# The query projection of a cross-attention as one Strassen step with streamed operands, in a fused decoder block on one Trainium2 core

## The chip, the cores and the metric

The program runs on one core of a Trainium2 chip. The metric is device time in microseconds of one execution, the median of the runs; the profile is one further execution with the hardware profiler on. The engines are TensorE (PE in the profile, its weight loads as PEld), VectorE (DVE), ScalarE (ACT), GpSimd (POOL) and SyncE (SP), whose queue issues nearly all DMAs.

## What is computed

A decoder block over 1024 tokens of width 1024 in float32: a mixer of a state-space branch and a gated linear attention branch, then cross-attention to 256 memory tokens, then a SwiGLU feed-forward layer, each behind an RMSNorm and with a residual sum. The part that matters here:

```python
merged = sigmoid(g_ssd) * (y_ssd @ w_up_ssd) + sigmoid(g_gla) * (y_gla @ w_up_gla)
h = h + merged @ w_o                       # 1024 x 1024
n = rmsnorm(h, norm_xattn)
q = (n @ w_xq).reshape(S, 4, 256)          # the query projection, 1024 x 1024
k, v = split(rmsnorm(mem, norm_mem) @ w_xkv, 2)
p = softmax(q @ k * 256 ** -0.5)
h = h + (p @ v) @ w_xo
```

## The kernel before

Activations lie transposed: 128 channels on the partitions, tokens along the free dimension, in two halves of 512 tokens (j = 0, 1). All matmuls of the projections are float32r with split operands: an operand x is kept as a rounded high part (a copy by ACT) and a low part (x minus the high part, by DVE), and a product is three matmuls, high x high, high x low and low x high. `split` makes such a pair, `into` makes one from a PSUM bank into an input slot.

Four dense 1024 x 1024 products of this part run one after another through `dense`: w_up_ssd, w_up_gla, w_o and w_xq, then, after the attention, w_xo. `dense(no, ins, post, pre)` runs over 8 blocks of 128 output channels and both token halves. Each of the 16 outputs is one PSUM bank ("acc", four of them) that takes 8 input blocks x 3 matmuls of 512 columns. The weights come from `Left` (lines 1190 to 1219): units of 256 output channels are loaded whole into "aux" buffers (1 MB each), and split, 128 channels at a time, into a ring of two buffers "wd" of the pool "m", two outputs ahead of use.

The output of w_o becomes the residual stream: `residual` adds the old one, stores it (h1_d), gives it to `put_xq` (lines 1365 to 1369) and squares it for the norm's statistics (`Stats.take`: the square on ACT into one buffer "sq", the running sum "ssum" on POOL or DVE, whichever of the two a meter kept at build time has free first). `put_xq` scales by the norm's gain and makes the high and the low part, the input i_xq of the query projection. The query projection writes its 8 output blocks, again split, into i_q, from which the attention takes scores. The factor of the norm itself, one number per token, is applied later, to the scores.

Beside the main work run side jobs, written as generators that `run` advances a step at a time. `presum` (lines 1297 to 1318) is the one that matters: it prepares sums of quadrants of w_ffn_out for the Strassen step of the last layer. Each of its 11 passes loads 1 MB into one buffer "pre" of the pool "m", makes four sums of 128 x 512 on POOL and stores each to down_d. It starts in the product of w_up_ssd and has steps until the query projection; down_d is read only by the down projection at the end.

Buffers of 8 KB per partition come from three pools by name: "op" (14), "aux" (4) and "m" (4). An input of a dense product takes 8 of them (`EVEN`: all "op"; `ODD`: six "op" and two "aux"). "ga" (6 of 2 KB) holds the residual's blocks and the raw keys and values. PSUM has 8 banks, four "acc" and four "bank".

The order on each queue is set at build time by a scheduler that follows the program's order as a priority and simulates the engines; work of a later step is drawn forward where its inputs and buffers are there. `ahead()` raises the priority of the instructions in it by 200 places. A queue then waits in order: an instruction that waits holds all that stand behind it on its engine.

The down projection of the feed-forward layer (lines 1568 to 1714) is already a Strassen step of the form that the change uses: seven products, in each of which both operands are streamed, and four banks filled side by side.

Of the kernel before, what the change touches and what calls it, by code (L numbers as in the profile page):

```python
# [10 lines left out]
F32R = mybir.dt.float32r  # L11
# [5 lines left out]
P = 128  # L17
# [61 lines left out]
def block_kernel(ctx: ExitStack, tc: tile.TileContext, t: dict, out: bass.AP):  # L79
# [19 lines left out]
    def dram(name, *shape):  # L99
        return dr.tile(list(shape), F32, name=name, tag=name)  # L100
# [14 lines left out]
    yg_d = dram("yg_d", D, TOK)  # L115
    act_d = dram("act_d", 7 * D_FF // 2, HALF)
    down_d = dram("down_d", 4 * D_FF // 2, HALF)
    kT_d = dram("kT_d", D, MEM)
    vm_d = dram("vm_d", MEM, D)
    cs_d = dram("cs_d", P, P)  # L120
# [1069 lines left out]
    class Left:  # L1190
# [2 lines left out]

        def __init__(s, mats):
            s.seq, s.raw, s.w, s.ring = [(W, u) for W in mats for u in range(4)], [], [], []

        def load(s, n):
            while len(s.raw) < min(n, len(s.seq)):
                W, u = s.seq[len(s.raw)]
                r = slot("aux", (P, NB, 256), name="raw")  # L1200
                SP.dma_start(r, W[:, 256 * u:256 * u + 256].rearrange("(k p) c -> p k c", p=P))
                s.raw.append(r)

        def upto(s, n):
            while len(s.w) < min(n, 2 * len(s.seq)):
# [12 lines left out]
            s.upto(n + 2)  # L1218
            return s.w[n]

    left = Left((t["w_up_ssd"], t["w_up_gla"], t["w_o"], t["w_xq"], t["w_xo"]))

    def paired(keys):

        return [(lambda k=k: slot(k, (P, 2, TOK), F32R, name="hl")) for k in keys]

    def hl(slots_, k):
        if callable(slots_[k]):
            slots_[k] = slots_[k]()
        return slots_[k]  # L1230

    def into(slots_, k, j, src, e=None):
        x = hl(slots_, k)
        split(src, x[:, 0, half(j)], x[:, 1, half(j)], e)
# [18 lines left out]
            yield  # L1253

    EVEN, ODD = ("op",) * 8, ("op",) * 6 + ("aux",) * 2
    i_ys, i_yg, i_wo, i_xq, i_q, i_xo = (paired(x) for x in (EVEN, ODD, EVEN, ODD, EVEN, EVEN))

    def fetch(src, dst, gain=None):

# [37 lines left out]
    def presum():  # L1297


        r = slot("m", (P, 2, D), name="pre")  # L1300
        for k in range(KP):
            SP.dma_start(r, t["w_ffn_out"][256 * k:256 * k + 256, :].rearrange("(j p) c -> p j c", p=P))
            yield
            a = lambda i, j: r[:, j, half(i)]
            s1_ = sums["m"].tile([P, HALF], F32, name="sa", tag="sa", bufs=2)
            put = lambda n, ap: SP.dma_start(down_d[(n * KP + k) * P:(n * KP + k + 1) * P, :], ap)
# [12 lines left out]

    def quad_of(src):  # L1320
        return lambda o, j: quad(src, o * P, 0, j)
# [35 lines left out]
    def residual(store, stats, gain, put, scale=1.0):  # L1357
# [4 lines left out]
            stats.take(j, q)  # L1362
        return post

    def put_xq(o, j, q, g):
        x = hl(i_xq, o)
        h, l = x[:, 0, half(j)], x[:, 1, half(j)]
        ACT.activation(h, q, AF.Copy, scale=g)
        DVE.scalar_tensor_tensor(l, q, g, h, ALU.mult, ALU.subtract)

    def waiting(g, n):
        for _ in range(n):
# [35 lines left out]
    drain(early)  # L1408
    load_kv(0)
    u_xo_stats = Stats(rp)  # L1410
# [126 lines left out]
    for n, _ in enumerate(dense(4, i_xo, residual(h2_d, u_xo_stats, "norm_ffn", put_xo), quad_of(h1_d), js=(1, 0))):  # L1537
# [213 lines left out]
```

## Time and profile before

| | |
|---|---|
| median of 3 runs | 1946.77 us (1946.58 to 1947.56) |
| span of the profiled execution | 1949.0 us |
| TensorE busy | 1916.2 us, 98% |
| DVE, ACT, POOL busy | 1298.5, 845.8, 557.8 us |
| moved by DMA | 317.98 MB, mean 163 GB/s |

The profile's page has the span and busy times, then groups of instructions by line, engine and operation (count, busy us, mean ns, and the idle time of the engine ahead of them with what ended it). L73 is the line of a helper through which all DVE and POOL instructions go, L51 the helper of all matmuls and L227 the one that makes high parts, so groups are told apart by their tiles: "hl" are split inputs, "wd" split weights of the dense products, "fs" split operands of the down projection, "pre" and "sa" the pre-sums. In a row of the order of time stand the start, the length, the engine, line and tiles, and in brackets how long the engine had idled and what ended that. All times in the trace are from the span's start. The query projection's matmuls lie between about 1075 and 1157 us.

### The profile page before, as it was taken

To read this page: it belongs to the slowest core of one execution; us is meant where nothing else is said; L and a number is where in the kernel's file an instruction comes from. 1 tells how busy PE (TensorE), PEld (TensorE's weight loads), DVE (VectorE), ACT (ScalarE), POOL (GpSimd) and SP (SyncE) were. 2 spreads that over 40 slices of the span, in tenths; PEclk is the share of its full clock that TensorE was granted. 3 is DMA by queue.
4 is the path that set the end of the run, shared out by engine and by line. 5 is a ranking of instruction groups with operands and counts; after the bars stand their busy time and mean duration, and the time that the engine had idled before them with its cause. 6 is when DMAs were issued, how large, how long until landed. Compare 5 with 4: busy or idle time off the path is not lost.

```text
span 1949.0 us, 26264 instructions
## 1 busy us (share of the span) xinstructions
PE 1916.2 (98%) x9776; PEld 1615.6 (83%) x9776; DVE 1298.5 (67%) x1873; ACT 845.8 (43%) x1485; POOL 557.8 (29%) x428
## 2 busy tenths in 40 slices
PE   7999999999999999999999999999999999999998
PEld 7998787888878888788887888888888888888888
DVE  7766879877776764655534237677777777766566
ACT  7534564655553444643223235444333333345243
POOL 0012334345543231022433000006445544320002
PEclk9999999999999999999999999999999999999999
DMA  9423383446553653997675201442233224177463
GB/s 341 144 93 101 130 307 107 152 161 186 174 173 123 198 167 124 348 346 270 226 269 164 82 22 44 140 141 82 90 126 110 82 100 144 42 271 239 157 224 126
DMA packets 237875, 317.98 MB, mean 163 GB/s; under 512 B 16538, under 2 KB 156036, under 8 KB 237748
## 3 DMA queue, kind: packets, MB, share of 16 engines
q1 hardware_dynamic: 236020, 310.01, 47.4%
q10 hardware_dynamic: 1728, 6.29, 0.8%
q8 instruction: 77, 1.26, 0.3%
q14 instruction: 50, 0.41, 0.1%
HBM read 215.27 MB, written 100.99 MB: 162 GB/s over the span
## 4 chain that ended last, share of the span: by engine, by line
PE 43%; DMA 3%; POOL 2%; DVE 1%; issue 1%; ACT 1%; POOLq 0%; SPq 0%; DVEq 0%; ACTq 0%
PE acc L51 38%; PE bank L51 4%; DMA pre<-in_w_ffn_out_dram 1%; POOL pre L73 1%; DMA down_d<-pre 1%; PE bank L55 1%; POOL ssum L73 0%; DVE hl L73 0%; POOL sa L73 0%; DMA h_d<-ga 0%; DMA ga<-vm_d 0%; DVE wd L73 0%; ACT wd L227 0%; ACT sq L493 0%; DVE phl L73 0%
## 5 line engine op out<-in xcount | busy, mean ns | idle before, releaser
L51 PE MATMUL acc<-hl,wd 128*128 128x512 f32 x1920 | 440.4, 390 | 3.6 <-DVE wd L73 2.0
L51 PEld LDWEIGHTS acc<-hl,wd 128*128 128x128 f32 x1920 | 359.6, 188 | 80.7 <-DVE wd L73 3.3
L73 DVE TENSOR_TENSOR wlo<-raw,whi 128x512 fp32r<-128x512 f32 x272 | 236.4, 875 | 103.6 <-ACT whi L227 103.5
L227 ACT ACTIVATE whi<-raw 128x512 fp32r<-128x512 f32 x272 | 169.5, 629 | 247.6 <-PE acc L51 201.0
L73 DVE TENSOR_TENSOR o<-acc,o 128x512 f32<-128x512 f32 (+1 forms) x256 | 172.6, 676 | 108.8 <-PE acc L51 95.4
L51 PE MATMUL acc<-fs 128*128 128x512 f32 (+1 forms) x792 | 155.7, 356 | 0.1
L51 PEld LDWEIGHTS acc<-fs 128*128 128x128 f32 x792 | 130.7, 189 | 20.8 <-issue 0.5
L73 DVE TENSOR_TENSOR fs<-fr,fs 128x1024 fp32r<-128x1024 f32 (+1 forms) x84 | 98.9, 1217 | 36.5 <-ACT fs L227 36.4
L227 ACT ACTIVATE fs<-fr 128x1024 fp32r<-128x1024 f32 (+1 forms) x84 | 79.2, 982 | 95.9 <-PE acc L51 31.2
L73 POOL TENSOR_TENSOR raw<-raw,sa 128x512 f32<-128x512 f32 x44 | 57.1, 1297 | 207.8 <-DVE wlo L73 207.8
L73 POOL TENSOR_TENSOR sa<-raw 128x512 f32<-128x512 f32 x43 | 69.6, 1619 | 107.0 <-DMA raw<-in_w_in_dram 78.9
L227 ACT ACTIVATE whi<-sa 128x512 fp32r<-128x512 f32 x96 | 59.6, 626 | 93.7 <-PE acc L51 92.3
L73 DVE TENSOR_TENSOR wlo<-sa,whi 128x512 fp32r<-128x512 f32 x96 | 80.9, 843 | 13.7 <-ACT whi L227 12.7
L73 DVE TENSOR_TENSOR wd<-raw,wd 128x1024 fp32r<-128x1024 f32 x40 | 52.8, 1323 | 47.6 <-ACT wd L227 47.2
L73 POOL TENSOR_TENSOR rstd<-rstd,mhalf 128x4 f32<-128x4 f32 (+1 forms) x7 | 8.7, 1246 | 257.0 <-DVE rstd L73 257.0
L227 ACT ACTIVATE wd<-raw 128x1024 fp32r<-128x1024 f32 x40 | 42.2, 1057 | 90.4 <-PE acc L51 89.8
L51 PE MATMUL acc<-T4h,whi 128*128 128x512 f32 x192 | 76.3, 397 | 2.4 <-DVE o L73 2.4
L51 PE MATMUL acc<-B22h,wlo 128*128 128x512 f32 x192 | 75.7, 394 | 1.5 <-DVE wlo L73 1.5
L51 PE MATMUL acc<-T1h,whi 128*128 128x512 f32 x192 | 76.3, 397 | 0.0
L51 PE MATMUL acc<-T2h,whi 128*128 128x512 f32 x192 | 75.9, 395 | 0.0
L51 PE MATMUL acc<-T3h,whi 128*128 128x512 f32 x192 | 75.9, 395 | 0.0
L51 PE MATMUL acc<-B22h,whi 128*128 128x512 f32 x192 | 75.7, 394 | 0.0
(399 smaller groups left out, 4698.6 us busy)
## 6 DMA issues: line engine op xcount, KB each, us to landing
raw<-in_w_in_dram SPq DMA_DIRECT2D x26, 1024.0 KB, 5.9
raw<-in_w_ffn_in_dram SPq DMA_DIRECT2D x22, 1024.0 KB, 6.5
act_d<-o SPq DMA_DIRECT2D x77, 256.0 KB, 2.1
fr<-act_d SPq DMA_DIRECT2D x35, 512.0 KB, 7.9
pre<-in_w_ffn_out_dram SPq DMA_DIRECT2D x11, 1024.0 KB, 10.0
fr<-down_d SPq DMA_DIRECT2D x20, 512.0 KB, 3.9
down_d<-pre SPq DMA_DIRECT2D x33, 256.0 KB, 3.1
h_d<-ga SPq DMA_DIRECT2D x32, 256.0 KB, 3.1
```

The lines of the kernel that those rows point to most:

```text
L51: return s.e.matmul(o, x, y, **kw)
L55: return s.e.transpose(o, x, i)
L73: return f(*a, **kw)
L227: ACT.activation(hi, src, AF.Copy)
```

## The change

The query projection is computed as one Strassen step (in Winograd's form) over quadrants of 512 x 512: seven products in place of eight, each with all 512 output channels of its half in four banks. w_xq is no longer one of `Left`'s matrices. The left operands are quadrants of w_xq or sums of them; the sums are made by `presum`, in four passes ahead of those over w_ffn_out, and stored in a new DRAM tensor xqs_d. The right operands are four quadrants of the input, which `put_xq` now stores unsplit in float32 (one scaled copy on ACT); DVE combines them in place, and both operands of every half product (two blocks of 128 channels) are split as they are needed, up to two half products ahead. Products that share terms add up in the same banks: B11, T2, T3 and T4 in four "acc" banks, T1 and B22 in four "bank" banks, B21 in four more. Three intermediate results are kept in "aux" buffers, and the four quadrants of the result go into i_q as before. `presum` is advanced two steps per half product in place of one per output. `Left` is held back at w_o's last unit until the twelfth step, when w_xo's units are freed.

```diff
+    xqs_d = dram("xqs_d", 2 * D, HALF)
...
+            s.limit = 12
...
-    left = Left((t["w_up_ssd"], t["w_up_gla"], t["w_o"], t["w_xq"], t["w_xo"]))
+    left = Left((t["w_up_ssd"], t["w_up_gla"], t["w_o"], t["w_xo"]))
...
-    i_ys, i_yg, i_wo, i_xq, i_q, i_xo = (paired(x) for x in (EVEN, ODD, EVEN, ODD, EVEN, EVEN))
+    i_ys, i_yg, i_wo, i_q, i_xo = (paired(x) for x in (EVEN, ODD, EVEN, EVEN, EVEN))
...
-        for k in range(KP):
-            SP.dma_start(r, t["w_ffn_out"][256 * k:256 * k + 256, :].rearrange("(j p) c -> p j c", p=P))
+        todo = [(t["w_xq"].rearrange("(j k p) c -> k p j c", j=2, p=P)[k], xqs_d, 4, k) for k in range(4)]
+        todo += [(t["w_ffn_out"][256 * k:256 * k + 256, :].rearrange("(j p) c -> p j c", p=P), down_d, KP, k)
+                 for k in range(KP)]
+        for src, dst, kn, k in todo:
+            SP.dma_start(r, src)
...
+    class Wide:
+        SEQ = ("B11", "T1", "B22", "T2", "B21", "T3", "T4")
+        LEFT = {"B11": (0, 0), "B21": (0, 1), "T1": 0, "B22": 3, "T2": 1, "T3": 2, "T4": (1, 1)}
+        COMB = {"T1": ((0, 0), (0, 1), (0, 0)), "T2": ((0, 0), (1, 1), (0, 0)), "T3": ((0, 1), (1, 1), (0, 1)),
+                "T4": ((1, 0), (1, 0), (0, 0))}
+        RIGHT = {"B11": (0, 0), "B22": (1, 1), "B21": (1, 0), "T1": (0, 0), "T2": (0, 0), "T3": (0, 1), "T4": (1, 0)}
...
+        def quad(s, i, j):
+            if (i, j) not in s.q:
+                s.q[i, j] = slot("op", (P, 4, HALF), name="rq")
+            return s.q[i, j]
...
+                r = slot(s.keys[len(s.raw)], (P, 4, HALF), name="wr")
+                SP.dma_start(r, w.rearrange("(k p) c -> p k c", p=P))
...
+        def prep(s, n):
+            while len(s.ops) < min(n, 14):
+                m, kp = divmod(len(s.ops), 2)
+                s.load(m + 1)
+                name, c = s.SEQ[m], slice(2 * kp, 2 * kp + 2)
+                x = [slot("op", (P, 2, 2, HALF), F32R, name="ws") for _ in range(2)]
+                with ahead():
+                    if name in s.COMB:
+                        o, a, b = (s.quad(*ij)[:, c] for ij in s.COMB[name])
+                        sub(DVE, o, a, b)
+                    split(s.raw[m][:, c], x[0][:, 0], x[0][:, 1])
+                    split(s.quad(*s.RIGHT[name])[:, c], x[1][:, 0], x[1][:, 1])
+                s.ops.append(x)
+        def evac(s, name, u, p):
+            with ahead():
+                if name in ("B11", "T1", "B22"):
+                    if name not in s.keep:
+                        s.keep[name] = slot(s.side, (P, 4, HALF), name="wk")
+                    ACT.activation(s.keep[name][:, u], p, AF.Copy)
+                elif name == "T4":
+                    s.post(1, 0, u, p)
+                else:
+                    k, i, j = {"T2": ("B22", 0, 1), "B21": ("B11", 0, 0), "T3": ("T1", 1, 1)}[name]
+                    o = s.keep[k][:, u]
+                    add(DVE, o, p, o)
+                    s.post(i, j, u, o)
+        def steps(s):
+            x = 0
+            for m, name in enumerate(s.SEQ):
+                if name in ("B11", "T1", "B21"):
+                    banks = [(acc if name == "B11" else bank)() for _ in range(4)]
+                    if name == "B11":
+                        s.chain = banks
+                elif name in ("T2", "T3", "T4"):
+                    banks = s.chain
+                fresh = name in ("B11", "T1", "B21")
+                for kp in range(2):
+                    s.load(m + 3)
+                    s.prep(x + 3)
+                    w, b = s.ops[x]
+                    for u in range(4):
+                        for k in range(2):
+                            for n, (a, c) in enumerate(((0, 0), (0, 1), (1, 0))):
+                                PE.matmul(banks[u], w[:, a, k, u * P:(u + 1) * P], b[:, c, k],
+                                          start=fresh and kp + k + n == 0, stop=kp + k == 2 and n == 2,
+                                          skip_group_check=True)
+                    x += 1
+                    if kp:
+                        for u in range(4):
+                            s.evac(name, u, banks[u])
+                    yield
+    xq = Wide(t["w_xq"], xqs_d, lambda i, j, u, p: into(i_q, 4 * i + u, j, p), ("aux", "op", "aux") * 3, "aux")
...
     def put_xq(o, j, q, g):
-        x = hl(i_xq, o)
-        h, l = x[:, 0, half(j)], x[:, 1, half(j)]
-        ACT.activation(h, q, AF.Copy, scale=g)
-        DVE.scalar_tensor_tensor(l, q, g, h, ALU.mult, ALU.subtract)
+        ACT.activation(xq.quad(o // 4, j)[:, o % 4], q, AF.Copy, scale=g)
...
-    run(dense(3, i_xq, lambda o, j, p, g: into(i_q, o, j, p)), (xq_side(), 1.0), (early, 1.0))
+    def next_left():
+        left.limit = len(left.seq)
+        left.upto(26)
+        yield
+    run(xq.steps(), (xq_side(), 1.0), (early, 2.0), (waiting(next_left(), 12), 1.0))
```

More of the change, by code (lines that the diff above doesn't have):

```diff
@@ L1195, in __init__ @@
             s.seq, s.raw, s.w, s.ring = [(W, u) for W in mats for u in range(4)], [], [], []
+            s.limit = 12
         def load(s, n):
-            while len(s.raw) < min(n, len(s.seq)):
+            while len(s.raw) < min(n, s.limit):
                 W, u = s.seq[len(s.raw)]
@@ L1204, in upto @@
         def upto(s, n):
-            while len(s.w) < min(n, 2 * len(s.seq)):
+            while len(s.w) < min(n, 2 * s.limit):
                 u, i = divmod(len(s.w), 2)
@@ L1305, in presum @@
             s1_ = sums["m"].tile([P, HALF], F32, name="sa", tag="sa", bufs=2)
-            put = lambda n, ap: SP.dma_start(down_d[(n * KP + k) * P:(n * KP + k + 1) * P, :], ap)
+            put = lambda n, ap: SP.dma_start(dst[(n * kn + k) * P:(n * kn + k + 1) * P, :], ap)
             add(POOL, s1_, a(1, 0), a(1, 1))
@@ L1363, in residual, with __init__, load @@
         return post
+    class Wide:
[4 more added lines that the diff above has]
+        RIGHT = {"B11": (0, 0), "B22": (1, 1), "B21": (1, 0), "T1": (0, 0), "T2": (0, 0), "T3": (0, 1), "T4": (1, 0)}
+        def __init__(s, W, sums_d, post, keys, side):
+            s.W, s.sums_d, s.post, s.keys, s.side = W, sums_d, post, keys, side
+            s.q, s.raw, s.ops, s.keep, s.chain = {}, [], [], {}, None
+        def quad(s, i, j):
+            if (i, j) not in s.q:
+                s.q[i, j] = slot("op", (P, 4, HALF), name="rq")
+            return s.q[i, j]
+        def load(s, n):
+            while len(s.raw) < min(n, 7):
+                src = s.LEFT[s.SEQ[len(s.raw)]]
+                if isinstance(src, tuple):
+                    i, j = src
+                    w = s.W[half(j), half(i)]
+                else:
+                    w = s.sums_d[half(src), :]
+                r = slot(s.keys[len(s.raw)], (P, 4, HALF), name="wr")
+                SP.dma_start(r, w.rearrange("(k p) c -> p k c", p=P))
+                s.raw.append(r)
+        def prep(s, n):
[19 more added lines that the diff above has]
+                    s.post(1, 0, u, p)
+                else:
+                    k, i, j = {"T2": ("B22", 0, 1), "B21": ("B11", 0, 0), "T3": ("T1", 1, 1)}[name]
[27 more added lines that the diff above has]
+                    yield
@@ L1536, in block_kernel @@
     B = Operands(b_xo, 4, order=("B11", "T1", "B21", "B22", "T2", "T3", "T4"))
-    for n, _ in enumerate(dense(4, i_xo, residual(h2_d, u_xo_stats, "norm_ffn", put_xo), quad_of(h1_d), js=(1, 0))):
+    for n, _ in enumerate(dense(3, i_xo, residual(h2_d, u_xo_stats, "norm_ffn", put_xo), quad_of(h1_d), js=(1, 0))):
         if n >= 8:
```

## The prediction, made before the changed kernel was run

> **What bounds the kernel now.** I read the page from the top, then the windows around the query projection, then TensorE in order of time there. Of the page, the span and the line of engines:
>
> ```profile
> span 1949.0 us, 26264 instructions
> PE 1916.2 (98%) x9776; PEld 1615.6 (83%) x9776; DVE 1298.5 (67%) x1873; ACT 845.8 (43%) x1485; POOL 557.8 (29%) x428
> ```
>
> Busy TensorE is not yet TensorE at its peak, so the stage itself has to be read. The windows give the stretch, then busy time of PE, weight loads, DVE, ACT and POOL with instruction counts, the granted clock, and DMA:
>
> ```profile
> 985.00:1073.00 88.00, 85.93 (x375) 69.90 (x375) 40.24 (x44) 29.80 (x44) 34.48 (x26) 1.00 0.64 212
> 1074.70:1156.50 81.80, 81.77 (x369) 67.98 (x369) 18.80 (x25) 17.11 (x25) 2.03 (x2) 1.00 0.18 60
> 1157.00:1222.00 65.00, 64.61 (x404) 57.09 (x402) 46.98 (x119) 38.28 (x102) 0.00 (x0) 1.00 0.10 33
> ```
>
> They are the output projection w_o, the query projection, and cross-attention. In the second PE never rests, DVE and ACT are under a quarter busy, and DMA is nearly idle. So the query projection lasts as long as its matmuls do. What one costs is its pitch, not its duration (389 ns in the groups, since neighbours overlap). From PE in order of time, the long run of that stage and one of the down projection:
>
> ```profile
> 1087.23 69.42 PE L51 MATMUL acc<-hl,wd 128*128 128x512 f32 x305
> 1779.58 60.00 PE L51 MATMUL bank<-fs 128*128 128x512 f32 x264
> ```
>
> 69.42/305 = 0.2276 us and 60.00/264 = 0.2273 us: the pitch is the same for both loop orders. I take 0.2273.
>
> **The change, part by part.**
>
> *Matmuls.* The direct product is 16 outputs x 8 blocks x 3 terms = 384 matmuls of 512 columns, 87.3 us. The Strassen step is 7 products x 4 output blocks x 4 blocks x 3 terms = 336, 76.4 us. That is **-10.9 us**, if TensorE stays fed. The down projection is the nearest row for the new loop: four banks at a time, both operands streamed, 264 matmuls without a gap.
>
> *Operands.* The prices, as minimum/median/maximum in ns, or count with busy us and mean:
>
> ```profile
> L227 ACT ACTIVATE wd<-raw x40: 1039/1061/1065, 800.8 to 1275.2; 128x1024 fp32r<-128x1024 f32 x40
> L73 DVE TENSOR_TENSOR wd<-raw,wd x40: 1211/1225/2319, 803.2 to 1276.3; 128x1024 fp32r<-128x1024 f32 x40
> L227 ACT ACTIVATE hl<-acc x16: 576/590/602, 1075.5 to 1157.4; 128x512 fp32r<-128x512 f32 x16
> L73 DVE TENSOR_TENSOR hl<-acc,hl x16: 679/686/692, 1076.1 to 1159.3; 128x512 fp32r<-128x512 f32 x16
> L73 DVE TENSOR_TENSOR gx<-gy 128x1024 f32<-128x1024 f32 x4 | 5.5, 1376 | 0.0
> L73 DVE TENSOR_TENSOR o<-acc,o 128x512 f32<-128x512 f32 x248 | 169.3, 684 | 98.2 <-PE acc L51 84.8 <-issue 13.3
> ```
>
> The 14 half products need 28 splits: 28 x 1.225 = 34.3 us of DVE and 28 x 1.061 = 29.7 of ACT. Four products combine two quadrants on DVE, twice each: 8 x 1.376 = 11.0. Evacuation adds 12 sums on DVE (8.2) and 12 copies on ACT (7.1); the 16 result splits stay (11.0 DVE, 9.4 ACT), and two splits of w_xo's weights (2.5 and 2.1). Sum: DVE 67.0 of 76.4 us (88%), ACT 48.3 (63%). So **DVE goes from a quarter to nearly full**, still under TensorE. What a stage like that costs shows near the start of the kernel, in the Strassen units of the input projection:
>
> ```profile
> 200.00:250.00 50.00, 48.34 (x212) 39.16 (x211) 43.62 (x43) 22.87 (x35) 21.77 (x23) 1.00 0.43 148
> 250.00:300.00 50.00, 49.17 (x217) 40.19 (x216) 40.51 (x43) 30.85 (x40) 18.34 (x12) 1.00 0.78 286
> 300.00:350.00 50.00, 49.69 (x219) 40.49 (x218) 45.30 (x48) 26.47 (x34) 15.99 (x9) 1.00 0.38 131
> 350.00:400.00 50.00, 49.28 (x246) 40.32 (x245) 41.77 (x48) 31.67 (x58) 21.27 (x14) 1.00 0.43 138
> ```
>
> DVE is 81 to 91% busy there, and PE loses 0.31 to 1.66 us per 50, 3.52 of 200 together. On 76.4 us that is 0.5 to 2.5 us; I take the mean, **+1.3**.
>
> *The side work moved to other stages.* In w_o's projection the second half of each operand split leaves DVE (line 1369, 16 instructions):
>
> ```profile
> L73 DVE SCALAR_TENSOR_TENSOR hl<-ga,cols,hl 128x512 fp32r<-128x512 f32 x16 | 18.8, 1175 | 23.6 <-ACT hl L1368 23.6
> ```
>
> That frees 18.8 us of DVE where it is only 46% busy (40.24 of 88), so I credit nothing. The pre-sums of POOL become 15 passes instead of 11. From POOL in order of time, the first instruction of the first and of the eleventh pass, and the group of the third and fourth sums:
>
> ```profile
> 833.98 1.28 POOL L73 TENSOR_TENSOR sa<-pre 128x512 f32<-128x512 f32 x1 [47.69 <-DMA pre<-in_w_ffn_out_dram]
> 1021.77 1.28 POOL L73 TENSOR_TENSOR sa<-pre 128x512 f32<-128x512 f32 x1 [7.53 <-DMA pre<-in_w_ffn_out_dram]
> L73 POOL TENSOR_TENSOR pre<-pre x22: 1272/1733/2359, 836.6 to 1025.6; 128x512 f32<-128x512 f32 x22
> ```
>
> Ten periods take 187.8 us, 18.8 each. The four passes over w_xq come first and end near 834 + 4 x 18.8 = 909, long before the second product wants them. The last pass over w_ffn_out ends at 1021.77 + 4 x 1.3 = 1027 now and slides to about 1027 + 4 x 18.8 = 1102, into the new stage. POOL gets 16 more sums (21 to 28 us), SP 20 more issues for the pre-sums and 3 more for operands at 0.3 to 0.4 us each, all behind one another on SP's queue; DMA carries 15 MB for w_xq instead of 4. At 60 GB/s and a share of 0.18 the stage has room for that. POOL's length alone costs nothing, since the sums are read only after 1755. What costs is who queues behind it:
>
> ```profile
> ACT sq L493 <- POOL ssum L73: 25.2, 4, 11.9
> ```
>
> That is, of the waits of this stage, four of ACT, 25.2 us in all, the longest 11.9. In order of time:
>
> ```profile
> 1028.18 0.63 ACT L493 ACTIVATE sq<-ga 128x512 f32<-128x512 f32 x1 [11.71 <-POOL ssum L73]
> 1028.89 1.29 POOL L73 TENSOR_TENSOR ssum<-ssum,sq 128x512 f32<-128x512 f32 x1 [0.74 <-ACT sq L493]
> ...
> 1030.75 1.04 ACT L227 ACTIVATE wd<-raw 128x1024 fp32r<-128x1024 f32 x1
> ...
> 1031.84 0.73 PE L51 MATMUL acc<-hl,wd 128*128 128x512 f32 x2 [0.38 <-ACT wd L227]
> ...
> 1033.34 21.60 PE L51 MATMUL acc<-hl,wd 128*128 128x512 f32 x94 [0.76 <-DVE wd L73]
> ```
>
> POOL waits in order for a pre-sum's load; a sum of squares stands behind it; ACT's next square has one buffer and waits 11.71 us; the weight split stands behind the square; PE loses 0.38 + 0.76 = 1.1 us. Two of the four waits are such long blocks, in passes 10 and 11 (25.2 us is little more than twice 11.9), and one reached PE. Passes 12 to 14 now fall on the rest of w_o's projection: 0 to 3.4 us more; I take one more block reaching PE at about two thirds, **+0.8**.
>
> *The hand-over.* Of 14 "op" buffers, w_o's input holds 8, the new quadrants 4, the second product's operand 1. The first pair of new operands wants 2, so one waits until w_o's last product has read its first block: 3 x 0.2273 = 0.7 us into 24 x 0.2273 = 5.5. Then ACT has the copy and the square of the output before (about 1.3 us), the split takes 1.06 + 1.23, ready at 4.3: 1.2 us to spare. Behind the waiting split on ACT stand the copies of w_o's last output and the next splits, and TensorE waits for all of them. No row shows this wait. Unblocked it costs 0, and it would also spare the 0.15 us that the old start lost; with an 11.7 us block it costs 11.7 - 1.2 = 10.5. I take **+1.0**, near the free end, since only part of a block has to meet a 5 us stretch.
>
> Later waits I cost at nothing: every accumulation bank is emptied while three others are filled (18 x 0.2273 = 4.1 us against 0.68), and attention needs the last quarter of the queries last, by which time its first heads keep PE busy (64.61 of 65 above).
>
> *Sum:* -10.9 + 1.3 + 0.8 + 1.0 = -7.8 us. The profiled execution's span is 1949.0, the median of the timed runs 1946.77, 0.1% apart, so I subtract from the median: **1939.0 us**.
>
> **The rivals.**
>
> *Everything is hidden.* -10.9 and the 0.15 of the old start: 1935.7. For it: the gapless run of the down projection. Against it: DVE has no combinations to make there.
>
> *The hand-over starves.* The ACT block above meets w_o's last outputs, and PE waits 5 to 10.5 us: 1946.77 - 10.9 + 2.1 + 5 to 10.5 = 1943.0 to 1948.5, the gain mostly given back. For it: the two long blocks of ACT above. Against it: the free end above, and that pre-sums wait less as DMA empties. The granted clock is 1.00 in all windows quoted. The Trainium skill, "TensorE: Matmul & The Clock Gate", What's actually happening, says that an idle window of about 3.4 us halves the array clock; by it a starved hand-over would cost some 1.7 us more (an estimate from that page), which no row here shows.
>
> *VectorE becomes the bound (slower).* A DVE instruction with both inputs in SBUF is stretched when POOL works beside it:
>
> ```profile
> 1039.08 1.43 POOL L73 TENSOR_TENSOR ssum<-ssum,sq 128x512 f32<-128x512 f32 x1 [0.81 <-ACT sq L493]
> 1039.29 1.77 DVE L73 SCALAR_TENSOR_TENSOR hl<-ga,cols,hl 128x512 fp32r<-128x512 f32 x1
> ...
> 1042.45 0.75 DVE L73 SCALAR_TENSOR_TENSOR hl<-ga,cols,hl 128x512 fp32r<-128x512 f32 x1 [0.79 <-ACT hl L1368]
> ```
>
> 1.77 instead of 0.75 us; the wide split likewise reaches 2319 against 1225 ns. If all 28 splits and 8 combinations paid 1.1 us, DVE would need 67.0 + 39.6 = 106.6 us, and the stage would last longer than the old 87.3: 1946.77 + 19.3 = 1966. It decides when over (87.3 - 67.0)/1.1 = 18 of the 36 pay. Against it: passes 13 to 15 at most overlap, 4 sums each, so at most 12 of the 36 pay, 13 us, DVE 80 us: 3.8 over TensorE's 76.4, and 1943 at worst. The Trainium skill, "SBUF — State Buffer", SBUF: two separate sides, states the same as a rule: such an instruction and a GpSimd one share a port pair under an exclusive lock, and the second waits for all of the first. The rows above agree with it (1.02 us lost beside a 1.43 us sum).
>
> *The saving is not there*: attention or the buffers of the last pre-sum hold what follows, within 0.2% of before. Attention's keys for the second head wait for the pre-sum's buffer, free near 1102, and attention, at 1156.5 now, starts near 1149.
>
> **How the numbers follow.** Forecast (1937 to 1942) 0.53, all hidden (below 1937) 0.14, starved hand-over 0.23, DVE bound 0.07, no saving 0.03. 0.2% of the time, 3.9 us, is about what a measurement of this kernel can tell from no change: faster is below 1942.9, slower above 1950.7. Forecast and hidden are faster, and half of the starved case (0.11): 0.78. Slower: 0.07. Same: 0.15. The range, 1935 to 1946, reaches to the hidden case and into the starved one and leaves out the slow rival.
>
> **What would show it.** PE's instructions fall by 48 to about 9728, at an unchanged pitch. The new stage has about 336 matmuls in 76 to 79 us with DVE near 88%. A gap of PE ahead of its first matmul, released by an operand's split, is the hand-over, and ACT waiting on POOL before it names the cause. Splits well over 1.3 us on average in that stage would mean the port, and pre-sums running past 1102 would make it worse. I would be wrong if PE shows several gaps over 1 us between products, or attention begins by waiting for its keys.

## The result, and the profile after

The changed kernel takes **1963.87 us** (median of 4 runs, 1961.87 to 1965.41) against 1946.86 us for the kernel before, measured beside it: a ratio of 1.0084, 95% interval 1.007 to 1.0098. It is slower by 17 us where 7.8 us faster was forecast, and above the range.

The page's span and engines, after:

```profile
span 1962.1 us, 26287 instructions
PE 1912.1 (97%) x9728; PEld 1609.8 (82%) x9728; DVE 1337.8 (68%) x1911; ACT 873.3 (45%) x1517; POOL 564.7 (29%) x430
```

The 48 matmuls are gone, so TensorE lost its time waiting or slowed. In the rows that follow, `rq` are the quadrants of the input, `wr` a left operand as it is loaded, `ws` the split operands, `wk` the intermediate results that are kept, `kvhl` the split keys and values of the attention (their raw form is loaded into `ga`), `pe` its probabilities and `phl` their split transposes. L228 is the line of the high parts in the changed kernel. TensorE in order of time, after, from the start of the dense products (start, length, group, and in brackets the idle time ahead and what ended it; each row is a run without a gap):

```profile
801.89 259.64 PE L51 MATMUL acc<-hl,wd 128*128 128x512 f32 x1144 [0.38 <-DVE wd L73]
1078.65 14.22 PE L51 MATMUL acc<-ws 128*128 128x512 f32 x48 [17.12 <-ACT ws L228]
1095.37 14.48 PE L51 MATMUL bank<-ws 128*128 128x512 f32 x48 [2.50 <-ACT ws L228]
...
1183.29 0.65 PE L55 MATMUL bank<-ident,pe 128*128 128x128 f32 x4 [1.22 <-DVE hl L73]
1184.71 0.65 PE L55 MATMUL bank<-ident,pe 128*128 128x128 f32 x4 [0.76 <-DVE hl L73]
```

The three products ahead run without a gap at the old pitch (259.64/1144 = 0.2270 us). The gap stands at the hand-over to the new stage: 17.12 us, and 2.50 one product later. And the products behind the gaps are long: 48 matmuls need 11.0 us at that pitch with the tail of the last one, and took 14.22 and 14.48. The windows, after (columns as in the prediction), show why, and then a stage that runs as worked out:

```profile
1061.50:1078.65 17.15, 0.03 (x2) 0.01 (x1) 4.25 (x7) 4.70 (x7) 5.50 (x4) 0.58 0.77 247
1078.65:1092.87 14.22, 14.22 (x48) 10.81 (x48) 11.11 (x9) 4.09 (x5) 8.95 (x4) 0.78 0.54 191
1092.87:1109.85 16.98, 14.42 (x49) 11.17 (x50) 15.97 (x16) 16.27 (x22) 0.00 (x0) 0.80 0.56 199
1110.00:1166.00 56.00, 56.00 (x257) 46.63 (x256) 38.85 (x49) 26.66 (x36) 2.00 (x2) 1.00 0.29 94
```

The granted clock is 0.58 in the gap and 0.78 and 0.80 in the two products behind, as means of these stretches; from 1110 it is 1.00 and PE never rests. In windows of 2 us it is 0.60 from 1064 to 1066 and 0.50 from there to 1084, then 1.00 from 1086 to 1094, 0.50 again from 1096 to 1100, and 1.00 from 1102. So TensorE ran at half its clock for some 6 us behind each of the two gaps, and the two slow products lost 3.2 and 3.4 us.

Who held the operand `ws`? ACT in order of time, after:

```profile
1041.16 0.62 ACT L494 ACTIVATE sq<-ga 128x512 f32<-128x512 f32 x1
1067.62 0.63 ACT L228 ACTIVATE kvhl<-ga 128x512 fp32r<-128x512 f32 x1 [25.84 <-DMA ga<-kT_d]
1071.81 0.63 ACT L228 ACTIVATE kvhl<-ga 128x512 fp32r<-128x512 f32 x1 [3.56 <-DMA ga<-vm_d]
1073.80 0.72 ACT L1459 ACTIVATE rq<-ga,cols 128x512 f32<-128x512 f32 x1 [1.36 <-DVE ga L73]
...
1077.55 1.04 ACT L228 ACTIVATE ws<-rq 128x1024 fp32r<-128x1024 f32 x1
...
1093.22 1.15 ACT L228 ACTIVATE kvhl<-ga 128x512 fp32r<-128x512 f32 x2 [10.12 <-DMA down_d<-pre]
```

ACT stood for 25.84 us at the split of the first head's keys, an instruction of the attention that the build-time order had put ahead of w_o's last outputs (`rq`) and of the first operand split (`ws`). The keys had not been loaded. Before, ACT stood at the same split too, but for 10.52 us, and TensorE idled 0.78 us behind it:

```profile
1053.45 0.63 ACT L227 ACTIVATE kvhl<-ga 128x512 fp32r<-128x512 f32 x1 [10.52 <-DMA ga<-kT_d]
```

SP in order of time, after, says why it became longer:

```profile
1049.56 0.32 SPq L1311 DMA_DIRECT2D down_d<-sa  x1
...
1053.55 0.87 SPq L1311 DMA_DIRECT2D down_d<-pre  x1
...
1061.72 0.38 SPq L1307 DMA_DIRECT2D pre<-in_w_ffn_out_dram  x1
1063.05 0.37 SPq L1478 DMA_DIRECT2D ga<-kT_d  x1
```

The load of the keys (L1478) stands behind the stores (L1311) and the next load (L1307) of the pre-sum passes. The waits of SP's queue between 985 and 1110 us (line and what it waited for: us in all, times, the longest):

```profile
SPq L1311 <- POOL sa L73: 22.1, 6, 6.0
SPq L1185 <- DMA h_d<-ga: 19.4, 5, 8.1
SPq L1311 <- POOL pre L73: 17.0, 19, 1.8
SPq L1307 <- DMA down_d<-pre: 10.9, 7, 4.2
```

SP waits for POOL's sums and for stores to land, in order, some 50 us of this stretch for the pre-sums alone. Before, the passes had ended by then, and the same load was issued at 1050.76:

```profile
1050.76 0.37 SPq L1388 DMA_DIRECT2D ga<-kT_d  x1
```

So the chain is: pre-sum on POOL, its store on SP, the keys' load behind it, the keys' split on ACT, the operands behind that, TensorE, and then the clock. The stretches between first matmuls of stages, each from the kernel's own profiled execution (us):

| | start to w_up_ssd | to the first score | to the end of w_xo | rest | span |
|---|---|---|---|---|---|
| before | 801.9 | 354.6 | 140.5 | 652.0 | 1949.0 |
| after | 799.4 | 366.6 | 144.1 | 652.0 | 1962.1 |

The second stretch holds 1488 matmuls in place of 1536 and grew by 12.0 us. **A second loss** of 3.6 us lies in the attention, whose work is the same: its first transposes wait 1.22 and 0.76 us (rows above), where before had one wait of 0.26:

```profile
1172.91 1.32 PE L55 MATMUL bank<-ident,pe 128*128 128x128 f32 x8 [0.26 <-DVE phl L73]
```

The spans differ by 13.1 us and the medians by 17.0. After's profiled run took 1.7 us more than its span; with as much, before's would lie 3.9 us above its median, so before's profiled execution is a long one.

### The profile page after: what moved, and what is told of

Its sections match the earlier page's. It is cut to its first block, busy times and chain, and to the rows that moved or that the text cites. A ratio compares the mean times of both kernels' runs of the same rounds, so it can differ in the third digit from the quotient of the medians.

```text
span 1962.1 us, 26287 instructions
## 1 busy us (share of the span) xinstructions
PE 1912.1 (97%) x9728; PEld 1609.8 (82%) x9728; DVE 1337.8 (68%) x1911; ACT 873.3 (45%) x1517; POOL 564.7 (29%) x430
## 5 line engine op out<-in xcount | busy, mean ns | idle before, releaser
L51 PE MATMUL acc<-hl,wd 128*128 128x512 f32 x1536 | 350.9, 390 | 1.8 <-ACT wd L228 1.4
L51 PEld LDWEIGHTS acc<-hl,wd 128*128 128x128 f32 x1536 | 287.5, 188 | 63.4 <-ACT wd L228 2.6
L228 ACT ACTIVATE whi<-raw 128x512 fp32r<-128x512 f32 x272 | 170.0, 630 | 250.8 <-PE acc L51 209.2
L228 ACT ACTIVATE fs<-fr 128x1024 fp32r<-128x1024 f32 (+1 forms) x84 | 79.5, 984 | 95.4 <-PE acc L51 29.7
L228 ACT ACTIVATE whi<-sa 128x512 fp32r<-128x512 f32 x96 | 59.8, 627 | 95.0 <-PE acc L51 93.7
L73 POOL TENSOR_TENSOR sa<-pre 128x512 f32<-128x512 f32 x15 | 20.7, 1377 | 213.9 <-DMA pre<-in_w_xq_dram 93.4
L51 PE MATMUL acc<-T3h,wlo 128*128 128x512 f32 x192 | 75.1, 391 | 0.0
```

What stands on the lines that cost most here:

```text
L51: return s.e.matmul(o, x, y, **kw)
L73: return f(*a, **kw)
L228: ACT.activation(hi, src, AF.Copy)
```

## The experiments

### Is it the buffers or the keys?

The prediction's hand-over was one of buffers. Two edits moved the key and value splits behind operand or result splits on ACT's queue, one in each kernel (in the changed one behind the tenth operand split, in the direct one behind the fifth result split of the query projection):

```diff
-        for i in range(2):
-            split(es[i], ...)
+        with ExitStack() as behind:
+            behind.enter_context(tc.issue_after(marks[KVX].ins))
+            for i in range(2):
+                split(es[i], ...)
```

> The changed kernel with one edit: the splits of the keys and values are queued on ACT behind the tenth operand split of the Strassen step, so that ACT can't wait for their loads ahead of w_o's last outputs and the first operands. Queue theory (ACT stood 25.8 us at the key split while the outputs of w_o and the first operand waited behind it, and again 10.1 us): both gaps of PE (17.1 and 2.5 us) and the low clock after them (about 6.7 us) go, about 26 us, and the time is 1936 to 1941. Buffer theory (the first operands wait for w_o's input buffers): the gap at the hand-over stays above 10 us, and the time above 1953. VectorE theory (the stage itself is too full): the first gap goes, but PE has new gaps between products, 1945 to 1955.

Measured: 1969.52 us, ratio 1.009 (1.0059 to 1.0122), far from the queue theory's 1936 to 1941. With the same buffers the hand-over was now without a gap, so the buffers are not what held it. But TensorE in order of time has one gap instead, and ACT's row names the next load in SP's queue:

```profile
1112.48 2.08 PE L51 MATMUL acc<-ws 128*128 128x512 f32 x4 [27.61 <-ACT ws L1416]
```

```profile
1110.42 1.06 ACT L228 ACTIVATE ws<-wr 128x1024 fp32r<-128x1024 f32 x1 [33.68 <-DMA wr<-xqs_d]
```

The streamed operand `wr` was loaded from 1104.43 on, behind two pre-sum passes. Taking the keys out of the way only moves the stall to whatever is next on that queue.

> The kernel before the change with only the key and value splits queued on ACT behind the fifth result split of the query projection. Queue theory: PE's idle time in w_o's product falls by the stall that a key split caused there (about 0.9 us of 2.1), so 0 to 2 us faster than before; it is what the same edit is worth without the change. If it gains over 5 us, the edit and not the Strassen step explains a fast run of the changed kernel with it.

Measured: 1946.6 us, ratio 0.9993 (0.998 to 1.0006): the direct kernel does not care where the keys are split.

### Is it the pre-sums?

First fewer passes, in the changed kernel (the last four over w_ffn_out are left out, and the down projection reads the sums of earlier rows in their place):

```diff
-                 for k in range(KP)]
+                 for k in range(KP - 4)]
...
-                w = down_d[(src * KP + k) * P:(src * KP + k + kn) * P, :].rearrange("(k p) c -> p k c", p=P)
+                w = down_d[(src * KP + k % 6) * P:(src * KP + k % 6 + kn) * P, :].rearrange("(k p) c -> p k c", p=P)
```

> The changed kernel without the last four of the eleven pre-sum passes over w_ffn_out (the down projection reads the sums of earlier rows in their place, at the same sizes), so that the pre-sums end about as early as before the change, near 1030. Theory that the longer pre-sums hold SP's queue and so the loads of the keys: the key split still stands in ACT's queue ahead of w_o's last outputs, but its load is issued some 12 us earlier, ACT waits 12 us or less, the second wait (for the pre-sum's buffer) goes, PE's gap is under 4 us, the time is 1937 to 1944. Theory that only the place of the key split in ACT's queue matters, with SP as late as before: the gap stays over 12 us, 1955 to 1964.

Measured: 1947.47 us, ratio 0.9992 (0.998 to 1.0004). 16 us came back, less than the theory asked for (1937 to 1944): the keys' load is issued at 1052.57 us, but ACT still stood 17.7 us there and not 12 or less, and a gap of 5.05 us is left in w_o's last product. Then more passes, in the direct kernel: the four over w_xq, whose sums nobody reads there.

```diff
+        todo = [(t["w_xq"].rearrange("(j k p) c -> k p j c", j=2, p=P)[k], xqs_d, 4, k) for k in range(4)]
+        todo += [(t["w_ffn_out"][256 * k:256 * k + 256, :].rearrange("(j p) c -> p j c", p=P), down_d, KP, k)
+                 for k in range(KP)]
```

> The kernel before the change (direct product) with four pre-sum passes over w_xq put ahead of the eleven, as in the change; their sums go unread. If the pre-sums hold up the key loads whatever the product is: ACT's wait at the key split grows from 10.5 us to 20 us or more, the weight splits behind it come late, and the time rises by 4 to 15 us over before. If the loss needs the Strassen step's own operands: within 2 us of before.

Measured: 1970.89 us, ratio 1.0108 (1.0081 to 1.0135). Four passes alone cost the direct product 23 us, without any Strassen step; 4 to 15 were expected, and by way of the keys, for which ACT waited 8.3 us and not 20. The path is another there. Its waits:

```profile
ACT sq L494 <- POOL ssum L73: 50.2, 8, 12.1
```

This is the block of the prediction, now eight times; and its largest gaps in TensorE's order of time:

```profile
1075.56 0.74 PE L51 MATMUL acc<-hl,wd 128*128 128x512 f32 x2 [4.41 <-ACT wd L228]
...
1092.79 12.29 PE L51 MATMUL acc<-hl,wd 128*128 128x512 f32 x45 [6.97 <-ACT hl L1372]
```

In the changed kernel the build put all 14 of these sums on DVE, and ACT has no wait for POOL between 985 and 1110 us; there the pre-sums' waits reached TensorE through SP instead. Next, all passes, but with their loads and stores issued from GpSimd's queue:

```diff
-            SP.dma_start(r, src)
+            nc.gpsimd.dma_start(r, src)
...
-            put = lambda n, ap: SP.dma_start(dst[...], ap)
+            put = lambda n, ap: nc.gpsimd.dma_start(dst[...], ap)
```

> The changed kernel with all DMAs of the pre-sums (loads and stores) issued from POOL's queue, the engine that makes the sums, in place of SP's; nothing else differs. Theory that the pre-sums stop SP's queue (SP stood 22 us for their sums and 11 us for their stores between 985 and 1110 us, with the key loads and the operand loads behind them): the first key load is issued before 1055, ACT's wait at the key split falls from 25.8 us to about 10 to 15 us, PE's gap at the hand-over to under 4 us, no PE gap over 2 us later, and the time is 1936 to 1946. Rival, the pre-sums' share of DMA bandwidth or of the port that DVE and POOL share is what counts, whatever queue issues them: the gaps stay within 5 us of 17.1 and 2.5, and the time above 1955.

Measured: 1947.12 us, ratio 0.9996 (0.9985 to 1.0007). The work is the change's, only the queue differs, and 16.8 us are gone; the hand-over has no gap. The keys' load is issued at 1046.13 us and ACT waits 3.4 us for it. The passes even end later than in the changed kernel (near 1111 us against 1091), so neither their length nor their bytes hold the stage up. The time is 1 us above the range expected, for the reason of the next section. So **the cause of the large loss is shown: the pre-sums' place in SP's queue.** The same move in the direct kernel:

> The kernel before, its eleven pre-sum passes on GpSimd's own queue. It is the direct product under the condition that freed the Strassen step. Theory A: the direct kernel has little to gain, some 2 us of the stretch of w_o, and may lose 4 us where the first pre-sum load comes early: 1945 to 1951, no gap over 1 us of PE between 985 and 1156. Theory B: the waits of ACT for pre-sums cost the direct kernel too, and it gains as much as the changed kernel did in that move: 1940 or below.

Measured: 1950.52 us, ratio 1.0017 (1.0009 to 1.0026): no gain, 3 us of loss. And own queue and later keys together in the changed kernel:

> Both edits: the pre-sums' DMAs on POOL's queue, and the key splits queued on ACT behind the tenth operand split. If both waits of ACT (for keys, for streamed operands) come from SP's queue, PE has no gap over 2 us between 985 and 1170, the granted clock is 1.00 throughout, and the time is 1934 to 1939, the full 10.9 us less at most 3 us. If DVE at nearly 90% is a bound of its own, PE still loses over 3 us between products and the time is 1940 or more.

Measured: 1948.6 us, ratio 1.0004 (0.9988 to 1.0021), where 1934 to 1939 was expected: the median shows nothing more to be had from the keys. The ten runs spread from 1945.65 to 1957.81 us, and the profiled one is the longest. In it a weight split of DVE (1.2 us elsewhere) took 5.33 us at 927.41 in the product of w_up_gla, beside three sums of GpSimd, and TensorE idled 4.63 us for it; e9 below has such blocks too.

### Why is it then only level?

With its own queue the new stage saves about what it should (343.0 us to the first score; the direct kernel has 354.6 in the long execution above and 350.9 in e4's), yet the time equals before. 5.0 us are lost in the attention (145.5 against 140.5). My first theory was the last product T4, whose four results come out together; here it runs output by output:

```diff
+                if name == "T4":
+                    s.prep(x + 2)
+                    for u in range(4):
+                        for kp in range(2):
+                            ...
+                        s.evac(name, u, banks[u])
```

> The changed kernel with the pre-sums on GpSimd's own queue, and its last product T4 run output block by output block (12 matmuls into one bank, then the next bank) instead of half product by half product. Theory A: attention begins late because T4's four results come out together, so that eight instructions of ACT and DVE (about 2.4 and 2.7 us) stand ahead of the softmax of the first head; one by one, three of the four are split while TensorE works, the waits of the first transposes (1.22 and 0.74 us) go, the stretch from the first score matmul to the last of w_xo falls from 145.2 to about 142, and the time from 1947.1 to about 1944.5. Theory B: the stretch is longer for another reason, the order that the build gives to attention's instructions or the keys that wait for the pre-sum's buffer: the stretch stays at 144 to 146 and the time at 1947.

Measured: 1946.22 us, ratio 0.9998 (0.9988 to 1.0008). The transposes wait 1.22, 0.74 and 0.27 us, as without the edit, and the stretch is 144.2, 1.3 us shorter and not the 142 expected: **that theory falls.** What the trace showed instead is when w_xo's units are loaded. SP in order of time, pre-sums on their own queue, and then before:

```profile
1119.73 0.37 SPq L1203 DMA_DIRECT2D raw<-in_w_xo_dram  x1
1127.54 0.37 SPq L1203 DMA_DIRECT2D raw<-in_w_xo_dram  x1
1132.21 0.37 SPq L1203 DMA_DIRECT2D raw<-in_w_xo_dram  x1
1222.76 0.38 SPq L1203 DMA_DIRECT2D raw<-in_w_xo_dram  x1
```

```profile
1115.30 22.13 SPq L1201 DMA_DIRECT2D raw<-in_w_xo_dram  x2
1211.98 0.38 SPq L1201 DMA_DIRECT2D raw<-in_w_xo_dram  x1
```

Three units ahead of the attention, not two. The new `next_left` asks for weights 24 and 25, and `upto` then loads two units ahead of them, through the third of w_xo. Each unit is one of four "aux" buffers, and the attention takes its probabilities (`pe`) and their split transposes (`phl`) from the same four. ACT in order of time in e5 shows a wait that fits a missing buffer: it stands ahead of the next probabilities and ends as the transposes of the ones before them do ("issue" means that the profile shows no releaser):

```profile
1158.55 0.56 ACT L1535 ACTIVATE pe<-acc,mx,xsc 128x256 f32<-128x256 f32 x1 [2.21 <-issue]
```

The edit, on top of the own queue and then on e2's kernel, which leaves out the same sums as there:

```diff
     def next_left():
-        left.limit = len(left.seq)
+        left.limit = 14
         left.upto(26)
...
+    left.limit = len(left.seq)
     for n, _ in enumerate(dense(3, i_xo, ...)):
```

> The changed kernel with the pre-sums on GpSimd's own queue, and with only two units of w_xo loaded in the query projection, as the kernel before has it, not three: the limit of the weight units is 14 in the twelfth step and is lifted behind the attention. Theory A: the third unit stands in one of the four aux buffers all through the attention, which needs them for the probabilities (pe) and their split transposes (phl), so that two heads' turns no longer overlap; with the buffer back the waits of the transposes (1.22, 0.74, 0.26 us) shrink to the 0.26 of before, the stretch from the first score matmul to the last of w_xo falls from 145.2 us to 140 to 141, and the time from 1947.1 to about 1942.5. Theory B: the loss in the attention comes from the results' order or from the keys: stretch 144 to 146, time about 1947.

Measured: **1941.8 us, ratio 0.9963 (0.9951 to 0.9976)**, the attention's stretch 140.0 us. TensorE in order of time, its gaps from 810 to 1310 us:

```profile
1135.49 11.16 PE L51 MATMUL acc<-ws 128*128 128x512 f32 x48 [1.63 <-DVE wk L73]
1167.42 1.22 PE L51 MATMUL acc<-kvhl,hl 128*128 128x256 f32 x8 [0.31 <-ACT kvhl L228]
```

The transposes wait no more, and the probabilities that stood 2.21 us in e5 follow at 1156.45 us without a wait. This version does all of the work and beats both kernels.

> The changed kernel without the last four of the eleven passes over w_ffn_out (the down projection reads sums of earlier rows in their place), pre-sums on SP's queue, and with two units of w_xo as above. It was 1947.5 with three units. Theory A: 145.4 us from the first score matmul to the last of w_xo becomes 140 to 141, and the time about 1943. Theory B: no change, 1947.

Measured: 1942.41 us, ratio 0.9971 (0.9959 to 0.9983); 145.6 us became 140.0. Is the attention's loss one of its own? The edit alone on the changed kernel, and the third unit in the direct one (`left.load(19)` ahead of the attention):

> The changed kernel with two units of w_xo in place of three, pre-sums on SP's queue as the change has them. Theory: the two losses are separate and add, so this one edit takes back the attention's part alone: stretch from the first score matmul to the last of w_xo 143.9 us down to 140 to 141, the gap of 17 us at the hand-over stays, time 1963.9 less 3 to 4 is about 1960. Rival: the attention's loss followed from the late pre-sums or the low clock after the gap, and then the stretch stays near 144 and the time at 1963 to 1964.

Measured: 1960.16 us, ratio 1.0061 (1.0049 to 1.0073). The hand-over keeps its gap and the attention has its time back:

```profile
1078.14 13.83 PE L51 MATMUL acc<-ws 128*128 128x512 f32 x48 [17.46 <-ACT ws L228]
```

> The kernel before, with the third unit of w_xo loaded at the end of the query projection. Theory: a third aux buffer held through the attention costs the direct kernel the same as the changed one: stretch from the first score matmul to the last of w_xo 140.3 us up to 144 to 145.5, transposes that wait 1.2 and 0.7 us for the values' splits, time 1946.7 plus 4 to 5 is 1951. Rival: the loss needs the Strassen step's late results beside it: stretch at 140 to 141, time 1947.

Measured: 1952.45 us, ratio 1.0029 (1.0019 to 1.0038), stretch 146.0 us, and its transposes wait, 2.23 us at once in place of the 1.2 and 0.7 expected:

```profile
1173.72 1.82 PE L55 MATMUL bank<-ident,pe 128*128 128x128 f32 x8 [2.23 <-DVE hl L73]
```

So it is a loss of its own, at home in either kernel. The stretches of all these (us):

| | start | to the first score | to the end of w_xo | span |
|---|---|---|---|---|
| e4, direct, keys later | 802.7 | 350.9 | 140.5 | 1946.7 |
| e3, direct, four more passes | 800.6 | 376.9 | 140.5 | 1970.0 |
| e15, direct, three units | 800.9 | 354.4 | 146.0 | 1953.3 |
| e2, fewer passes | 800.6 | 347.8 | 145.6 | 1945.8 |
| e5, own queue | 803.2 | 343.0 | 145.5 | 1944.3 |
| e12, own queue, two units | 803.3 | 343.2 | 140.0 | 1939.1 |
| e14, two units alone | 798.6 | 366.6 | 140.0 | 1957.2 |

### The gap at the start, and a run that got worse

With the own queue the first matmul of w_up_ssd comes 3 to 4 us later than after's, behind a gap of 3.9 to 4.3 us where the kernels with the pre-sums on SP's queue have 0.6 to 1.0: GpSimd's queue starts the first pre-sum load near 785 us, beside the product's own input. In e9 that one load stays on SP's queue.

```diff
-            nc.gpsimd.dma_start(r, src)
+            (SP if src is todo[0][0] else nc.gpsimd).dma_start(r, src)
```

> The changed kernel with the pre-sums on GpSimd's own queue, but the load of the first pass left on SP's queue, where it stands behind the loads of the product of w_up_ssd. Theory A: the gap of 4.31 us ahead of that product (first matmul at 803.2 us, 799.4 in the changed kernel) came from the first pre-sum load, which GpSimd's queue starts before the product's own input has landed: the gap goes, the first matmul is at 799 to 800, and the time falls from 1947.1 to about 1943.5. Theory B: the gap is the run to run spread of the loads there: the first matmul is anywhere from 799 to 804 and the time stays within 2 us of 1947.

Measured: 1960.45 us, ratio 1.0054 (1.0033 to 1.0074). The start is at 800.0, with 1.01 us of wait, as foreseen, but the time is 13 us above e5's. The six runs lie between 1949.82 and 1962.69 us, and the profiled one is among the long ones. In it the passes end near 1129 us (1111 in e5) and meet the stage's splits. TensorE, then DVE, then GpSimd in order of time:

```profile
1131.87 12.76 PE L51 MATMUL acc<-ws 128*128 128x512 f32 x47 [5.26 <-DVE ws L73]
1149.87 12.55 PE L51 MATMUL acc<-ws 128*128 128x512 f32 x48 [5.23 <-DVE wk L73]
```

```profile
1121.33 0.68 DVE L73 TENSOR_TENSOR wk<-acc,wk 128x512 f32<-128x512 f32 x1
...
1123.13 6.42 DVE L73 TENSOR_TENSOR hl<-wk,hl 128x512 fp32r<-128x512 f32 x2
1129.47 1.21 DVE L73 TENSOR_TENSOR ws<-wr,ws 128x1024 fp32r<-128x1024 f32 x1
```

```profile
1124.69 1.28 POOL L73 TENSOR_TENSOR pre<-sa,pre 128x512 f32<-128x512 f32 x1
1125.91 1.29 POOL L73 TENSOR_TENSOR pre<-pre 128x512 f32<-128x512 f32 x1
...
1127.72 1.27 POOL L73 TENSOR_TENSOR pre<-pre 128x512 f32<-128x512 f32 x1
```

Two small subtractions of DVE (low parts of results, 0.68 us each alone) took 6.42 us, until GpSimd's last sum had ended. The operand splits stood behind them, and that is the gap of 5.26 us; the causes of the other gaps of this run were not taken apart. It fits the port of the prediction's rival, in one long block in place of many short ones; no run takes it apart from other causes.

> Both edits together, the first pre-sum load on SP's queue and T4 output by output. If both theories A hold the savings add: about 1941 us, first matmul of w_up_ssd at 799 to 800, stretch from the first score matmul to the last of w_xo 142 us. If only one holds, 1944 to 1945.

Measured: 1956.08 us, ratio 1.0053 (1.0034 to 1.0073): the start is at 800.8 us and most of e9's loss stays. The 3 us of the start come from that one load, as e9 and e11 show; an order that has neither cost was not tried.

## Why the prediction was wrong, step by step

**The matmuls: right.** 9728, at the old pitch. e12 shows the saving: 79.9 us from the first `ws` matmul to the first score, of which 76.4 us are the 336 matmuls, 1.7 the norm's 16 small ones and 1.6 the one gap. The old stage is longer than the window that the prediction gave it: 384 matmuls at 0.2273 us cannot lie in 81.80 us, and it began near 1067 us, not 1075. The -10.9 does not hang on that.

**VectorE: right.** 67.0 us of DVE were worked out for the stage, with 1.3 us lost; e12 has 66.4 us there (83% of a longer stage) and one gap of 1.63, released by DVE:

```profile
1066.57:1146.49 79.92, 78.29 (x354) 64.77 (x352) 66.40 (x70) 45.24 (x61) 28.19 (x11) 1.00 0.38 129
```

The rival that VectorE bounds the stage falls for the changed kernel; e9 shows that its port is real when the passes end later.

**The pre-sums: the step that failed.** The step is the wait that longer pre-sums put on SP's queue, which the prediction counted at nothing. It wrote "POOL's length alone costs nothing, since the sums are read only after 1755. What costs is who queues behind it", and then looked behind POOL alone, at ACT's square: +0.8 us. That path does not exist in the changed kernel, whose sums of squares are on DVE. It listed 20 more issues on SP "at 0.3 to 0.4 us each, all behind one another", and priced the issuing, not the waiting: each store waits for its sum and each load for the stores, with all of SP's queue behind. The rest of SP's list, the keys and the streamed operands, does not enter the sum. By e2 and e5 this term is 16 to 18 us, and e3 shows 23 in the direct kernel by the path over ACT. The passes ended 11 us sooner than forecast (1091 against 1102), so their end was not what was mis-sized.

**The hand-over: right place, wrong cause and size.** +1.0 was forecast for buffers; 17.12 + 2.50 us of gap and 6.6 of slow clock were measured, and e1 has the same buffers and no gap there. The rival of a starved hand-over had the right kind of block, an ACT that waits, at 5 to 10.5 us; but ACT waited for the keys' DMA and not for POOL. The keys of the second head do wait for the pre-sum's buffer, as the prediction said under its last rival (10.12 us of ACT at 1093.22). It expected that in the attention, though; in ACT's queue the split stands between two operand splits, 70 us earlier.

**"Later waits I cost at nothing": wrong** by 3.6 us in the changed kernel and 5 to 5.6 where the stage ahead is clean. Of the reasons given, the late queries held, as e8 shows. The banks did not quite: T4 adds into T3's banks, and DVE's sums out of them stood behind weight and operand splits, so the first began at 1134.66 us in e12, 0.8 us behind T3's last matmul. That is the gap of 1.63 us. What was missed is the third unit in `next_left`, which stood in the diff.

**The clock.** The one rule cited gave 1.7 us for a starved hand-over. The Trainium skill, "TensorE: Matmul & The Clock Gate", What's actually happening, puts the halving behind an idle window of about 3.4 us. The trace agrees that the clock halves in the gap of 17.12 us (0.50 from 1066 on). It differs in two things. The clock was back at 1.00 from 1086 to 1094 and halved again behind a gap of only 2.50 us. And it stayed at half for some 6 us behind each gap, so that 3.2 and 3.4 us were lost, twice the estimate for each.

**The sum.** Without the two losses, 7.2 us are gained (0.9963 of the 1948.53 measured beside it), against the 7.8 forecast. That these are so near is in part luck: e12 pays some 3 us at the start that the forecast did not have, and nothing of its +0.8 and +1.0. The terms of the stage itself, -10.9 + 1.3 = -9.6, stand beside about -10 in e12 with those 3 us put back (an estimate from the gaps at the start). So they were sound, and the two things outside the stage made the sign.

## What to carry to other kernels

When side work gets longer, read the whole list of every queue that it issues on, its DMAs first: a store that waits for a sum holds each load behind it, and the price is paid by the engine whose in-order queue has the consumer of that load. When a change moves a prefetch, count the buffers of its pool that are held through the next stage, since a unit loaded early costs nothing in its own stage and can take double buffering from the next one. A gap of TensorE has to be priced with the slow matmuls behind it, here 6.6 us on 19.6.

## What the runs showed of the hardware that was not expected

GpSimd's sums can stand still for long while VectorE works. One sum of 1.28 us took 17.19 us in e5, while DVE ran SBUF-to-SBUF splits nearly back to back from 1073 to 1088 us; it ended 1.15 us behind the start of DVE's first pause (1088.75):

```profile
1072.71 17.19 POOL L73 TENSOR_TENSOR sa<-pre 128x512 f32<-128x512 f32 x1 [6.20 <-DMA pre<-in_w_ffn_out_dram]
```

The Trainium skill, "SBUF — State Buffer", SBUF: two separate sides, calls the port pair an exclusive lock that one instruction holds to its end. The rows agree that the loser waits, here past a dozen instructions of the other engine and not one; in e9 it was DVE that lost, 5 us. Five of the six changed kernels with the own queue have such a sum (17.19 to 20.17 us). It is not always so: in the changed kernel between 1082 and 1090 us the two took turns, GpSimd's sums at 2.2 to 2.3 us each beside DVE's splits at 2.3. What decides between the two the runs do not show.

A short gap of TensorE behind warm matmuls cost next to nothing (48 matmuls took 11.16 us behind 1.63 us in e12), while 5.23 us cost 1.5 (12.55 for 48, e9) and 2.50 us cost 3.4 (14.48 for 48, in the changed kernel). The length of a gap alone does not give its price.
